# Seven-product pairs in twos with plain pairs between, nine with raw kept sums, and another order of the down-projection

## The chip, the cores and the metric

The kernel runs on one core of a Trainium2 chip. The metric is the device time of one execution in microseconds, as the median over runs. Everything is float32 at the inputs and outputs. TensorE (PE) multiplies; VectorE (DVE), ScalarE (ACT) and GpSimd (POOL) do the rest; SyncE (SP) issues most of the DMAs, and POOL some of them.

## The reference, cut to what matters

One residual block over 512 tokens of width 1024: two attention branches, their gates and projections, and then a gated convolutional feed-forward. The change touches the feed-forward, whose hidden width is 2816, and work that prepares it earlier.

```python
def conv_glu(x, w_up, conv_w, conv_b, w_down):
    hid = x @ w_up
    hid = lax.conv_general_dilated(
        hid, conv_w[:, None, :], window_strides=(1,),
        padding=((CONV_WIDTH - 1, 0),),
        dimension_numbers=('NWC', 'WIO', 'NWC'),
        feature_group_count=2 * D_FF) + conv_b
    gate, up = hid[..., :D_FF], hid[..., D_FF:]
    return (jax.nn.silu(gate) * up) @ w_down
...
        x = x + (jax.nn.sigmoid(gate_a) * (out_a @ w_branch_a[l])
                 + jax.nn.sigmoid(gate_b) * (out_b @ w_branch_b[l])) @ w_out[l]
        x = x + conv_glu(rms_norm(x, norm2_g[l]), w_ffn_up[l], ffn_conv_w[l],
                         ffn_conv_b[l], w_ffn_down[l])
```

## The kernel before

**Products in three parts.** Every float32 operand of a matmul is split into a rounded high part (a cast by ACT) and a low part (a subtraction by DVE), and each product is made as high x high + high x low + low x high. So one block of a product is three matmuls, and every weight that comes in costs a cast and a subtraction (split_gen, lines 249/250 and 278/283; split_down, lines 168/172).

**Stages.** Up to about 312 us: input projections, attention A and B, with projections as filler. Then the branch projections (yB), w_out (wo) and the second norm. From about 388 us the up-projection, from 604 us the down-projection.

**Up-projection.** The 2816 hidden columns are 22 pairs up0 to up21; pair j holds 128 gate columns and the 128 up columns that belong to them. Pairs 0 and 1 (up_first) run in halves of 256 tokens. A plain pair (up_body) is 2 x 8 x 3 = 48 matmuls of 512 columns. Twelve pairs, listed in SEVEN, are made by seven block products in place of eight (up_seven, a Strassen scheme on 2 x 2 blocks: tokens left and right, input features upper and lower half, gate and up). Each of the seven is 12 matmuls of 256 columns, so 84. The products are made in the order b1, b5, b7, b6, b1, b5, b7; after the first three ACT copies the bank into pc (L1187, L1191, L1195) so that the bank can be added to later, and DVE adds the pieces into hu and hg (L1197 to L1214). The last two matmuls of a plain pair that stands ahead of a seven-product pair are held back and run a few matmuls later (L998, L999).

The scheme needs sums of token blocks (token_sums, tiles ts, made once during pair 1) and sums of weight blocks. park_gen makes the four weight sums of each pair during attention, yB and wo: four additions on DVE (L214), then stores to a DRAM tile, parked. For a pair in SUMS the four sums are stored raw (4 DMAs of 256 KB). For another pair three of them are split first (L224 on ACT, L225 on DVE) and stored as high and low parts (7 DMAs). One call of park() makes one step, and 44 calls are spread over the attention steps, two after every group of yB and wo. In the up-projection fetch_extra brings the sums back (L237, SP's queue): 6 DMAs for a split pair; 3 for a raw one, which split_seven then splits (L249, L250). The sums go alternately into the tiles wxh/wxl and, for pairs in SECOND, w2h/w2l. split_gen fetches pair j's sums one pair early if the tile's last user stands at least three pairs before; otherwise it fetches them when the split of pair j itself begins.

**Block sums for the down-projection.** Two pairs of the up-projection form a block pair i (0 to 10). After the odd one, up_fin calls pair_sums(i): four additions on DVE, and a list rest_ with the splits into ax and ay, done by ACT and POOL's accumulating DMAs (by_dma) and followed for i < 7 by a store of ay to ayd. rest_ waits in owed until pay() is called at a fixed place of a later pair. The tile ub, from which it reads, has room for four pairs, so pair 2i + 4 writes where block pair i was. Block pairs 0 and 1 give up their ax tiles: they are stored in axd (after pairs 6 and 9) and loaded again (L1249) after pair SECOND[-1] + 1 and after the last seven-product pair + 1.

**Down-projection.** Also a seven-product scheme. A first sweep (s = 0) runs over the 11 block pairs with four products each (24 matmuls of 512 columns per block pair, L1282), a second with three (18). The weights of step i come as wd0[i] and wd1[i], one step ahead.

**What sets the order.** The program is written in one order, and a planner with a simulated timeline arranges each engine's instructions; with tc.high_priority lifts some, and behind(...) fixes the order of two. Each engine then runs its own queue in order. So a wait holds up everything behind it on its engine.

Of the kernel before, what the change touches and what calls it, by code (L numbers as in the profile page):

```python
# [15 lines left out]
P = 128  # L16
# [6 lines left out]
NP = NF // 2  # L23
# [42 lines left out]

CUTS = ((0, 256, 512, 1024, 1536, 2048), (0, 512, 1024, 1536, 2048))

SEVEN = (4, 5, 7, 8, 10, 11, 13, 14, 16, 17, 18, 20)
SUMS = (11, 13, 14, 16, 17, 18, 20)  # L70
SECOND = (5, 8, 11, 14, 17)


@with_exitstack
def block_kernel(ctx: ExitStack, tc: tile.TileContext, x, xt, params, g2, rbx, wts, wd0, wd1, out):
# [47 lines left out]
    order = [key for key, _, _ in CHUNKS]  # L123

    pos = {k: i for i, k in enumerate(order)}
    raws, splits, extras, late = {}, {}, {}, {"halves": (), "casts": (), "products": (), "pcs": ()}
    FIRST_DN = order.index("dn0_0")
    keep = {}

    def load(i):  # L130
# [15 lines left out]
        if is_seven(i):  # L146
            n = SEVEN.index(i - pos["up0"])
            SP.dma_start(raw[:, 0:512], wts[i, :, 0:512])
# [44 lines left out]
    def is_seven(i):  # L193
        return i < len(order) and order[i] in [f"up{j}" for j in SEVEN]

    def park_gen():

        for m, j in enumerate(SEVEN):
            n = SEVEN.index(j)
            i = pos[f"up{j}"]  # L200
# [779 lines left out]
    pairs = {}  # L980
# [105 lines left out]
    def up_fin(j, pg, pu, g=None):  # L1086
        if g is None:
            g = gate(j, pg)
        u = ub[:, j % 4, :]
        conv(pu, NF + j, u)  # L1090
        late["fin"] = (V.tensor_tensor(u, g, u, op=ALU.mult),)
        if j % 2 == 1 and j // 2 < 9:
            steps = pair_sums(j // 2)
            steps[0]()

            def rest_(i=j // 2):
                for step in steps[1:]:
                    step()
                if i < 7:
                    G.dma_start(ayd[i], pairs[i][1].bitcast(F32))  # L1100
            owed.append(rest_)
            if j == 17:
                owed.pop()()

    owed = []

# [2 lines left out]
    def pay():  # L1109
        if owed:  # L1110
            owed.pop()()

    def up_body(j):
        def body(hi, lo):
            pg, pu = BANK(f"pg{j}", j - 1), BANK(f"pu{j}", j - 1)
            yield from up_mm(pg, hi, lo, 0, 0, S)
            g = gate(j, pg)
            held = [] if j + 1 in SEVEN else None
            yield from up_mm(pu, hi, lo, P, 0, S, held)

            def end():
                for mm in held or ():
                    late["flip"] = (behind(mm(), late["flip"]),)
                up_fin(j, pg, pu, g)
            if held:
                late["end"] = end
            else:
                end()
            if j % 2 == 0 and j + 1 not in SEVEN:
                pay()  # L1130
        return body

# [32 lines left out]
    def up_seven(j):  # L1165
        def body(hi, lo, wh, wl):
            b1, b5, b7, b6 = [BANK(f"p{n}_{j}", j - 1 + i // 2)[:, 0:256] for i, n in enumerate((1, 5, 7, 6))]
            left, right = slice(0, 256), slice(256, 512)
            pc = fp.tile([P, 3, 256], F32, tag="pc", name=f"pc{j}")
            hg = fp.tile([P, S], F32, tag="hg", name=f"hg{j}")  # L1170
            hu = fp.tile([P, S], F32, tag="hu", name=f"hu{j}")

            def prod(ps, w, b, h, first=True, last=True):
                for k in range(4):
                    sh, sl = w[0][:, 4 * b + k, :], w[1][:, 4 * b + k, :]
                    for n, (st, mv) in enumerate(((sh, h[0]), (sh, h[1]), (sl, h[0]))):
                        mm = PE.matmul(ps, st, mv[:, k, :], start=first and k == 0 and n == 0,  # L1177
                                       stop=last and k == 3 and n == 2, skip_group_check=True)
                        behind(mm, late["pre" if late.get("end") else "flip"])
                    if late.get("end"):  # L1180
                        late["flip"] = (mm,)
                        late.pop("end")()
            r, w = (hi, lo), (wh, wl)
            B = lambda a, q: [t[:, 4 * a:4 * a + 4, q] for t in (hth, htl)]
            prod(b1, r, 0, B(0, left), last=False)
            with tc.high_priority(60):
                late["pcs"] = (A.copy(pc[:, 0], b1),)  # L1187
            yield
            prod(b5, w, 0, ts[1], last=False)
            with tc.high_priority(60):  # L1190
                late["pcs"] = (A.copy(pc[:, 1], b5),)  # L1191
            yield
            prod(b7, r, 1, ts[3], last=False)
            with tc.high_priority(60):
                third = A.copy(pc[:, 2], b7)  # L1195
            late["pcs"] = (third,)
            V.tensor_tensor(pc[:, 1], pc[:, 1], pc[:, 2], op=ALU.add)  # L1197
            yield
            if j % 2 or j + 1 not in SEVEN:
                late["copied"] = (third,)  # L1200
                pay()
            prod(b6, w, 1, ts[2])
            V.tensor_tensor(hu[:, left], b6, pc[:, 0], op=ALU.add)
            V.tensor_tensor(hu[:, right], hu[:, left], pc[:, 1], op=ALU.add)
            yield
            prod(b1, r, 2, B(1, left), first=False)
            A.copy(hg[:, left], b1)
            yield
            prod(b5, w, 2, B(1, right), first=False)
            V.tensor_tensor(hg[:, right], b5, hu[:, left], op=ALU.add)  # L1210
            g = gate(j, hg)
            yield
            prod(b7, r, 3, ts[4], first=False)
            V.tensor_tensor(hu[:, left], b7, hu[:, left], op=ALU.add)  # L1214
            up_fin(j, None, hu, g)
            yield
        return body


    halves = []  # L1220
# [19 lines left out]
    for j in range(NF):  # L1240
# [5 lines left out]
        if j in (SECOND[-1] + 1, SEVEN[-1] + 1):  # L1246
            i = int(j == SEVEN[-1] + 1)
# [20 lines left out]
    def product(s, p, i, hi, lo, ts=(0, 1)):  # L1268
        if p in ON:
            banks[p] = banks[ON[p]]  # L1270
        elif p not in banks:
            banks[p] = [ptile(tag, BUFS[tag], f"P{p}_{t}") for t, tag in enumerate(SLOTS[p])]
        a = pairs[i][s]
        h = a.shape[-1] // 2
        first, last = i == 0 and p not in ON, i == NP - 1
        for t in ts:
            o = 256 * OP[p] + P * t
            sh, sl = a[:, o:o + P], a[:, h + o:h + o + P]
            mh, ml = hi[:, BLK[p], :], lo[:, BLK[p], :]
            dst = banks[p][t]  # L1280
            for st, mv, n in ((sh, mh, 0), (sh, ml, 1), (sl, mh, 2)):
                chain("products", PE.matmul(dst, st, mv, start=first and n == 0, stop=last and n == 2,  # L1282
                                            skip_group_check=True))
# [119 lines left out]
def _layout(inputs):  # L1403
    import numpy as np
    f = {k: np.asarray(v) for k, v in inputs.items()}
    x = f["x"]
    g = f["q_norm_g"][0]
    k = f["k_norm_g"][0]
    params = np.concatenate([
        f["norm1_g"].reshape(NK, P), np.concatenate([g, g])[None], np.concatenate([k, k])[None],  # L1410
        f["ffn_conv_w"].reshape(3 * 2 * NF, P), f["ffn_conv_b"].reshape(2 * NF, P)], axis=0).T

    idx = np.clip(np.arange(639) - 127, -128, 128) + 128
    rbx = f["rel_bias"][0][:, idx]
    wts = np.empty((len(CHUNKS) - 2 * NP, P, 2048), np.float32)
    for i, (key, kn, parts) in enumerate(CHUNKS[:-2 * NP]):
        views = [f[name][0][r0:r0 + kn * P, c0:c0 + n] for name, r0, c0, n in parts]
        w = views[0] if len(views) == 1 else np.concatenate(views, axis=1)
        if key in [f"up{j}" for j in SEVEN]:

            a = w.reshape(2, 4, P, 2, P).transpose(0, 3, 2, 1, 4)
            wts[i] = np.concatenate([a[k, f].reshape(P, 512) for k in range(2) for f in range(2)], axis=1)
            continue
        wts[i] = w.reshape(kn, P, 2048 // kn).transpose(1, 0, 2).reshape(P, 2048)
        if i < 2:

            wts[i] = np.concatenate([wts[i][:, a:b].ravel() for a, b in zip(CUTS[i], CUTS[i][1:])]).reshape(P, 2048)

    w = f["w_ffn_down"][0].reshape(NP, 2, P, 2, 512)
    wd0 = np.concatenate([w[:, 0, :, 0], w[:, 1, :, 0], w[:, 0, :, 1], w[:, 1, :, 1]], axis=2)  # L1430
    wd1 = np.concatenate([w[:, 1, :, 1], w[:, 1, :, 0]], axis=2)
    arrays = {"x": x, "xt": x[0].T.reshape(NK, P, S),
              "params": params, "g2": f["norm2_g"], "rbx": rbx, "wts": wts, "wd0": wd0, "wd1": wd1}
    return {n: np.ascontiguousarray(a) for n, a in arrays.items()}
# [15 lines left out]
```

## Time and profile before

| | |
|---|---|
| median of 3 runs | 714.71 us (714.57 to 2534.47) |
| profiled execution | 714.89 us, span 713.1 us |
| up-projection, 402 to 604 us of the span | PE 201.9 us busy, DVE 171.6, ACT 138.9 |
| down-projection, 604 to 709 us | PE 105.0 us busy, DVE 88.4, ACT 46.5 |
| DMA in the whole span | 150.78 MB, 211 GB/s in the mean |

The span is from the first to the last instruction of the profiled execution, and the time given beside it has what lies around. Matmuls are pipelined, so their busy times overlap: how close PE is to its limit is read from the distance of their starts, which the chain of waits gives by its long rows (start, length, number of matmuls). A row of a group of instructions reads: line, engine, operation, written tile <- read tiles, shape, count | busy us, mean ns of one | idle time before it and what ended it.

### The profile page before, as it was taken

The numbers are of one execution on the slowest core, as the hardware profiler recorded it, in microseconds if no ns is written. First come the engines' busy times: TensorE is split into PE (matmuls) and PEld (weight loads), VectorE is DVE, ScalarE is ACT, GpSimd is POOL, SyncE is SP. The second block draws the span as 40 slices with busy tenths as digits, with TensorE's granted clock in tenths as the row PEclk, the third lists the DMA queues.
The fourth block names the chain that finished last, engine by engine and source line by source line (L and its number), as shares of the span: only waits on it lengthen the run. The fifth ranks groups of instructions, "written<-read, shape, count | busy, mean of one in ns | idle before, by whom it ended". The sixth has DMA issues, their size and how long they took to land.

```text
span 713.1 us, 11229 instructions
## 1 busy us (share of the span) xinstructions
PE 707.7 (99%) x4091; PEld 621.9 (87%) x4091; DVE 589.2 (83%) x1049; ACT 433.2 (61%) x803; POOL 81.6 (11%) x115
## 2 busy tenths in 40 slices
PE   9999999999999999999999999999999999999997
PEld 7889998888988888888889989999898988888886
DVE  6668878787999999769567988688878998989687
ACT  6576656567776776534236667677768875544531
POOL 2501200000121211000000001120222121000000
PEclk9999999999999999999999999999999999999999
DMA  8722235444434383585966647997878799564563
GB/s 315 270 99 89 78 131 183 187 162 147 179 134 162 126 296 125 206 306 195 359 232 212 229 194 222 323 314 257 259 198 253 233 265 401 209 229 168 178 214 118
DMA packets 46999, 150.78 MB, mean 211 GB/s; under 512 B 5344, under 2 KB 8032, under 8 KB 39136
## 3 DMA queue, kind: packets, MB, share of 16 engines
q1 hardware_dynamic: 40032, 131.57, 52.1%
q0 software_dynamic: 6624, 18.35, 10.0%
q8 instruction: 32, 0.52, 0.3%
q14 instruction: 23, 0.19, 0.1%
q10 hardware_dynamic: 288, 0.14, 0.1%
HBM read 114.39 MB, written 28.31 MB: 200 GB/s over the span
## 4 chain that ended last, share of the span: by engine, by line
PE 89%; DMA 4%; issue 3%; DVE 2%; ACT 1%; SPq 0%; POOL 0%; DVEq 0%; POOLq 0%; ACTq 0%
PE P L1282 15%; PE p L1177 10%; PE vA L437 3%; PE uA L437 3%; PE gB L307 2%; PE gB L308 2%; PE qkB L309 2%; PE qkB L307 2%; PE gB L309 2%; PE pg L307 2%; PE qkB L308 2%; PE pg L309 2%; PE pg L308 2%; PE wo L307 2%; PE wo L309 2%
## 5 line engine op out<-in xcount | busy, mean ns | idle before, releaser
L172 ACT CAST whi_dn<-raw_dn 128x1024 fp32r<-128x1024 f32 x33 | 34.3, 1050 | 25.4 <-PE P L1282 16.7
L1282 PE MATMUL P<-whi_dn,ax 128*128 128x512 f32 x144 | 44.5, 389 | 0.0
L168 DVE TENSOR_TENSOR wlo_dn<-raw_dn,whi_dn 128x1024 fp32r<-128x1024 f32 x33 | 40.0, 1223 | 5.1 <-ACT whi_dn L172 5.0
L1282 PE MATMUL P<-whi_dn,ay 128*128 128x512 f32 x132 | 40.8, 389 | 0.0
L741 POOL TENSOR_SCALAR_AFFINE_SELECT bB<-bB 128x128 f32<-128x128 f32 x32 | 21.8, 686 | 143.6 <-DVE bB L740 134.4
L214 DVE TENSOR_TENSOR pkr<-pkr 128x512 f32<-128x512 f32 x40 | 27.4, 685 | 8.4 <-DMA pkr<-in_wts 4.2
L1177 PE MATMUL p<-ts,whi_up 128*128 128x256 f32 x192 | 34.1, 277 | 0.0
L307 PE MATMUL pg<-hth,whi_up 128*128 128x512 f32 (+1 forms) x96 | 33.9, 354 | 0.0
L309 PE MATMUL pg<-hth,wlo_up 128*128 128x512 f32 (+1 forms) x96 | 33.9, 353 | 0.0
L308 PE MATMUL pg<-htl,whi_up 128*128 128x512 f32 (+1 forms) x96 | 33.8, 353 | 0.0
L250 DVE TENSOR_TENSOR wlo_up<-raw_up,whi_up 128x1024 fp32r<-128x1024 f32 x24 | 29.0, 1219 | 3.5 <-ACT whi_up L249 3.5
L1282 PEld LDWEIGHTS P<-whi_dn,ax 128*128 128x128 f32 x144 | 27.0, 188 | 5.6
L308 PE MATMUL pu<-htl,whi_up 128*128 128x512 f32 (+1 forms) x90 | 31.5, 350 | 0.0
L307 PE MATMUL pu<-hth,whi_up 128*128 128x512 f32 (+1 forms) x90 | 31.5, 350 | 0.0
L309 PE MATMUL pu<-hth,wlo_up 128*128 128x512 f32 (+1 forms) x90 | 31.4, 349 | 0.0
L1282 PEld LDWEIGHTS P<-whi_dn,ay 128*128 128x128 f32 x132 | 24.8, 188 | 5.1
L1177 PEld LDWEIGHTS p<-ts,whi_up 128*128 128x128 f32 x192 | 29.0, 188 | 0.1
L739 DVE TENSOR_TENSOR_SCAN aB<-aB,reset 128x127 f32<-128x127 f32 (+3 forms) x32 | 25.9, 816 | 2.6 <-ACT aB L734 2.5
L1282 PE MATMUL P<-wlo_dn,ax 128*128 128x512 f32 x72 | 28.0, 389 | 0.0
L1177 PE MATMUL p<-hth,whi_up 128*128 128x256 f32 x96 | 26.7, 278 | 0.1
L249 ACT CAST whi_up<-raw_up 128x1024 fp32r<-128x1024 f32 x24 | 24.6, 1051 | 3.5 <-PE pu L308 2.8
L1177 PE MATMUL p<-hth,wlo_up 128*128 128x256 f32 x96 | 26.5, 276 | 0.0
(349 smaller groups left out, 2537.9 us busy)
## 6 DMA issues: line engine op xcount, KB each, us to landing
parked<-pkr SPq DMA_DIRECT2D x45, 256.0 KB, 2.7
raw_dn<-in_wd SPq DMA_DIRECT2D x11, 1024.0 KB, 4.9
pkr<-in_wts SPq DMA_DIRECT2D x10, 1024.0 KB, 6.9
raw_up<-in_wts SPq DMA_DIRECT2D x10, 1024.0 KB, 5.7
raw_up<-in_wts SPq DMA_DIRECT2D x12, 512.0 KB, 6.9
raw_dn<-in_wd SPq DMA_DIRECT2D x11, 512.0 KB, 3.6
wxl_up<-parked SPq DMA_DIRECT2D x21, 256.0 KB, 5.6
ayd<-ay POOLq DMA_DIRECT2D x7, 768.0 KB, 7.1
```

The costliest lines, as they stand in the source:

```text
L168: chain("halves", V.tensor_tensor(o, x, y, op=op))
L172: chain("casts", A.copy(hi[:, sl], src))
L214: V.tensor_tensor(b[o], b[x], b[y], op=op)
L249: behind(A.copy(h[:, sl], src[:, sl]), late["pcs"])
L250: V.tensor_tensor(l[:, sl], src[:, sl], h[:, sl].bitcast(F32), op=ALU.subtract)
L307: ins = PE.matmul(ps, sh, mh, start=first, stop=False)
L308: PE.matmul(ps, sh, ml, start=False, stop=False)
L309: PE.matmul(ps, sl, mh, start=False, stop=last)
L437: PE.matmul(pss[t], st[:, 4 * half + k, t * P:(t + 1) * P], mv[:, k, :], start=half == 0 and k == 0 and j == 0, stop=half == 1 and k == 3 ...
L739: V.tensor_tensor_scan(ar, ar, reset[:, S - n:S - 1][:, ::-1], 1.0, op0=ALU.mult, op1=ALU.max)
L1177: mm = PE.matmul(ps, st, mv[:, k, :], start=first and k == 0 and n == 0, stop=last and k == 3 and n == 2, skip_group_check=True)
L1282: chain("products", PE.matmul(dst, st, mv, start=first and n == 0, stop=last and n == 2, skip_group_check=True))
```

## The change

Three edits. The twelve seven-product pairs are put at other places: always two in a row with a plain pair between, then 18 and 20 alone. Nine of them keep raw sums in place of seven (SUMS), so three are split ahead in place of five; SECOND follows the new places. The conditions under which rest_ is paid follow the new places, and the call that paid it at once after pair 17 goes. In the down-projection a table DOWN puts block pair 2 ahead of 0 and 1; the host lays the weights out in that order. The number of seven-product and of plain pairs stays, and so does every product.

```diff
-SEVEN = (4, 5, 7, 8, 10, 11, 13, 14, 16, 17, 18, 20)
-SUMS = (11, 13, 14, 16, 17, 18, 20)
-SECOND = (5, 8, 11, 14, 17)
+SEVEN = (3, 4, 6, 7, 9, 10, 12, 13, 15, 16, 18, 20)
+SUMS = (7, 9, 10, 12, 13, 15, 16, 18, 20)
+SECOND = (4, 7, 10, 13, 16)
+
+
+DOWN = (2, 0, 1, 3, 4, 5, 6, 7, 8, 9, 10)
...
-    raws, splits, extras, late = {}, {}, {}, {"halves": (), "casts": (), "products": (), "pcs": ()}
+    raws, splits, extras, late = {}, {}, {}, {"halves": (), "casts": (), "products": (), "pcs": (), "flip": ()}
...
             owed.append(rest_)
-            if j == 17:
-                owed.pop()()
...
-            if j % 2 == 0 and j + 1 not in SEVEN:
+            if j == 18 or j < 18 and j % 2 == 0 and j + 1 not in SEVEN:
                 pay()
...
-            if j % 2 or j + 1 not in SEVEN:
+            if j == 18 or j < 18 and (j % 2 or j + 1 not in SEVEN):
                 late["copied"] = (third,)
                 pay()
...
-        a = pairs[i][s]
+        a = pairs[DOWN[i]][s]
...
-    w = f["w_ffn_down"][0].reshape(NP, 2, P, 2, 512)
+    w = f["w_ffn_down"][0].reshape(NP, 2, P, 2, 512)[list(DOWN)]
```

## The prediction

> **What bounds the kernel now.** I read the page first (shares of the span, then the slices), then the chain of work that ended last, then who makes TensorE's weight loads wait, and last the busy times by stretch.
>
> ```profile
> span 713.1 us, 11229 instructions
> PE 707.7 (99%) x4091; PEld 621.9 (87%) x4091; DVE 589.2 (83%) x1049; ACT 433.2 (61%) x803; POOL 81.6 (11%) x115
> ```
>
> The profiled execution took 714.89 us, so 1.8 us lie around its span of 713.1; the median of the runs shown is 714.71, 0.18 lower. PE is busy for all but 5.4 us. Busy matmuls can still be far apart, so the chain has to show whether they follow each other without gaps:
>
> ```profile
> 423.21 0.35 PE p L1177 x3
> 424.04 18.71 PE p L1177 x165
> 453.19 0.35 PE p L1177 x3
> 454.02 18.71 PE p L1177 x165
> ...
> 524.79 10.58 DMA wxl_up<-parked
> ...
> 548.79 0.35 ACT pc L1187
> 549.18 20.99 PE p L1177 x180
> 570.41 2.73 PE p L1177 x24
> ...
> 604.28 104.94 PE P L1282 x462
> 709.25 0.42 DVE x__7105 L1287
> ```
>
> In the double of seven-product pairs 4 and 5 (from 424.04) 165 matmuls of 256 columns take 18.71 us, 113.4 ns each. In the down-projection 462 matmuls of 512 columns take 104.94 us, 227.1 ns each. Twice the columns cost twice the time, so PE streams columns without a break. A seven-product pair (84 matmuls) is 84 x 113.4 = 9.5 us, a plain pair (48 of 512 columns) 48 x 227.1 = 10.9 us. The one stretch that isn't clean begins at 549.18, inside pair 16 of the run 16, 17, 18: 180 matmuls should take 18.71 + 15 x 0.1134 = 20.41 us and take 20.99, 0.58 us too long. Just before it, the last matmul before 549.18 starts at 548.81 and should have been followed 0.11 us later: 0.26 us more.
>
> ```profile
> 548.81 0.28 PE L1177 MATMUL p<-ts,wxl_up 128*128 128x256 f32 x1
> 549.18 0.39 PE L1177 MATMUL p<-hth,whi_up 128*128 128x256 f32 x1
> ```
>
> ```profile
> PEld gA L307 <- DVE mixA L626: 0.5, 1, 0.5
> PEld P L1282 <- DVE wlo_dn L168: 0.3, 1, 0.3
> PEld p L1177 <- ACT pc L1187: 0.3, 1, 0.3
> ```
>
> These waits agree: in the whole up-projection only one is listed, for ScalarE's copy of the first product (pc, L1187). So what the change can win there is about 0.58 + 0.26 = 0.84 us, and everything else must come from matmuls that it does not remove.
>
> **The change part by part.**
>
> *TensorE's work.* Twelve pairs by seven products before and after, ten plain ones before and after; the diff touches no product. The sum is 0. The pairs stand as 3 4 | 6 7 | 9 10 | 12 13 | 15 16 | 18 | 20 in place of 4 5 | 7 8 | 10 11 | 13 14 | 16 17 18 | 20, so there is one more turn from a plain to a seven-product pair. At such a turn three matmuls of 256 columns and the two held ones of 512 stand between 423.21 and 424.04: 3 x 0.1134 + 2 x 0.2271 = 0.79 us in 0.83. One more turn: +0.04 us.
>
> *The run of three goes.* The stall at 548.81 is the end of a delay of the helpers, not of PE: ScalarE sat for the kept sums of pair 16, whose transfer took 10.58 us (524.79 in the chain).
>
> ```profile
> ACT wxh_up L249 <- DMA wxl_up<-parked: 6.3, 2, 5.4
> wxl_up<-parked SPq DMA_DIRECT2D x21, 256.0 KB, 5.6
> w2l_up<-parked SPq DMA_DIRECT2D x15, 256.0 KB, 8.8
> ```
>
> After the change the last pairs are 15 16, plain 17, 18, plain 19, 20. Pair 18 then has another non-SECOND pair (15) three places before it, so the rule in split_gen fetches its sums early; in the old order 16 stood two places before and the fetch had to wait. The rest_ of block pair 8 is no longer forced out at once after pair 17, between two seven-product pairs, but paid in 18. What is late next is unknown; the doubles at 424.04 and 454.02, with the same 165 matmuls in 18.71 us, show that a double between plain pairs runs clean. I take all of it: -0.84 us; the bounds are -0.84 and 0 (the loss only moves).
>
> *Two more pairs keep raw sums* (9 for 7; parked already split are 3, 4, 6 for 4, 5, 7, 8, 10).
>
> ```profile
> L225 DVE TENSOR_TENSOR pkr<-pkr,pkh 128x512 fp32r<-128x512 f32 x10 | 6.9, 686 | 0.5 <-ACT pkh L224 0.3
> L224 ACT CAST pkh<-pkr 128x512 fp32r<-128x512 f32 x10 | 6.2, 620 | 6.0 <-DMA parked<-pkh 3.6 <-DVE pkr L225 2.1 <-DVE pkr L214 0.3
> L250 DVE TENSOR_TENSOR wxl_up<-wxl_up,wxh_up 128x1024 fp32r<-128x1024 f32 x4 | 4.9, 1221 | 4.6 <-ACT wxh_up L249 4.6
> L250 DVE TENSOR_TENSOR wxl_up<-wxl_up,wxh_up 128x512 fp32r<-128x512 f32 x4 | 2.7, 685 | 0.0
> L249 ACT CAST wxh_up<-wxl_up 128x1024 fp32r<-128x1024 f32 x4 | 4.2, 1046 | 5.4 <-DMA wxl_up<-parked 5.4
> L249 ACT CAST wxh_up<-wxl_up 128x512 fp32r<-128x512 f32 x4 | 2.5, 619 | 0.9 <-DMA wxl_up<-parked 0.9
> ```
>
> Removed from the attention stage: 2 x 3 casts of 0.62 (3.7 us of ACT), 2 x 3 subtractions of 0.686 (4.1 us of DVE), 2 x 3 stores of 256 KB on SP's queue, and four calls of park(), so the last sums are ready two groups earlier. Added in the up-projection: 2 x (1.221 + 0.685) = 3.8 us of DVE, 2 x (1.046 + 0.619) = 3.3 us of ACT. Removed there: 2 x 3 fetches of 256 KB on SP's queue (1.5 MB, 5 to 6 us at the 276 GB/s of the stretch below). The cover for the added work:
>
> ```profile
> 200.00:220.00 20.00, 20.00 (x104) 16.85 (x104) 19.90 (x38) 14.43 (x33) 3.58 (x6) 1.00 0.41 152
> 402.00:432.00 30.00, 30.00 (x171) 26.27 (x170) 26.63 (x42) 17.23 (x27) 0.73 (x1) 1.00 0.48 176
> 432.00:604.00 172.00, 171.90 (x1223) 160.22 (x1223) 144.92 (x226) 121.71 (x206) 33.67 (x43) 1.00 0.90 276
> 604.00:709.00 105.00, 105.00 (x464) 86.53 (x462) 88.39 (x115) 46.52 (x58) 1.05 (x2) 1.00 0.54 188
> ```
>
> The columns are stretch, length, busy PE, PEld, DVE, ACT, POOL, clock, DMA share and GB/s. From 432 to 604 DVE has 172 - 144.92 = 27.1 us free, 23.3 with the added 3.8; ACT has 50.3, 47.0 after. The DMA engines, 0.90 busy, are relieved. If that cover were gone, each microsecond of it would stop PE; with it, 0. In the attention stage DVE is full (19.90 of 20 at 200 to 220) and loses 4.1 us there, but the first three parked pairs are split as before, so the 0.5 us wait of gA L307 near 121 us stays, and PE shows no other wait for DVE there. I take -0.1, between 0 and -0.9 (that engine's lateness may hide in many small gaps).
>
> *Sevens begin one pair earlier.* Pair 3 starts at about 423.2 - 10.9 = 412.3 and needs the token sums and its own fetched sums.
>
> ```profile
> L237 SPq DMA_DIRECT2D w2l_up<-parked x15: 319/430/1409, 392.3 to 532.3; - x15
> L1161 DVE TENSOR_TENSOR ts<-x,ts x4: 1214/1216/1224, 394.7 to 403.6; 128x1024 fp32r<-128x1024 f32 x4
> 413.68 2.36 DVE L250 TENSOR_TENSOR wlo_up<-raw_up,whi_up 128x1024 fp32r<-128x1024 f32 x2 [2.29 <-ACT whi_up L249]
> 428.60 1.22 DVE L250 TENSOR_TENSOR wlo_up<-raw_up,whi_up 128x1024 fp32r<-128x1024 f32 x1
> ```
>
> The last token sum starts at 403.6 and takes 1.2 us, 7.5 us before 412.3: 0. The sums of the first two such pairs are fetched as soon as the feed-forward pool exists (the second pair's from 392.3, landing 8.8 us later), for 3 and 4 now in place of 4 and 5, and all is there by about 404: 0. Pair 3 by seven products adds five DVE steps of 0.42 us, 2.1 us, to 402 to 432, where DVE is free for 3.4 us, of which 2.29 are spent waiting at 413.68 for the weight buffer. So 1.0 us of the 2.1 may not fit. Pair 5's last split ends at 428.60 + 1.22 = 429.8, and PE reached pair 5 at about 423.2 + 0.5 + 9.5 = 433.2 (pair 4 and the two held matmuls): 3 us of slack against 1.0. I take 0; the bounds are 0 and +2.1.
>
> *pay() and the first-half sums.* rest_ for pairs 0 to 8 is paid in 3, 4, 7, 9, 10, 13, 15, 16, 18 (2, 5, 7, 8, 11, 13, 14, 17, 17 before): the same steps on ACT and POOL, two of them in one double at 3 4, 9 10 and 15 16, as before in 7 8 and 13 14. 0 on PE. Where it adds a wait it is on ACT, which writes ub again one pair later; behind it stand pc's copies, which PE needs three products (36 x 0.1134 = 4.1 us) after they are due.
>
> *Down-projection.* Block pair 2 is read first; it was never stored away. Block pairs 0 and 1 come back by a load:
>
> ```profile
> L1249 SPq DMA_DIRECT2D ax0b<-axd x1: 319/319/319, 561.9 to 561.9; - x1
> L1249 SPq DMA_DIRECT2D ax1b<-axd x1: 319/319/319, 586.7 to 586.7; - x1
> DMA to landing us min/median/max: 5.0/5.0/5.0
> ```
>
> ax0b has landed 37 us before the first product at 604.28, and ax1b 18 us before the second block pair (24 matmuls of 0.2271 us later, 609.7). Taking pair 2 first gives each one or two steps more of slack that was not needed: 0 us. The weights are put in the same order on the host, outside the time.
>
> The sum against the profiled execution: 714.89 + 0.04 - 0.84 - 0.1 = 713.99, about 714.0 us. I keep 714.0 for the median; the 0.18 between the two lies inside the range.
>
> **A rule to weigh.** The Trainium skill (Perfetto Trace Analysis, Identifying the Most-Contended Engine) says that TensorE's matmul busy share is no measure of its headroom and that the busy share of weight loads is. By that rule PE's 87% leaves 713.1 - 621.9 = 91 us; by the row of 104.94 us for 462 matmuls it leaves nothing in the down-projection, where weight loads are busy for only 86.53 of 105 us. The measured spacing decides here, and the rule is the ground of the rival on the fast side.
>
> **The rivals.**
>
> (B) The loss only moves. The delayed transfer of kept sums hits another double, with raw sums now also in 7, 9, 10. For it: 0.90 of the DMA time is used, and two rest_ still fall in one double. Against it: 1.5 MB less is fetched, and pair 16's neighbour 18 is gone. Time: 714.89 + 0.04, up to 0.3 more: 714.6 to 715.2. The change would then do nothing that shows.
>
> (C) A new wait in the first double, the case of the other sign. DVE comes out of the token sums late, and 1.0 to 2.1 us of its work does not fit before pair 5; PE waits for the second half of pair 5's weights or for a bank. It decides once the lateness passes the 3 us of slack above. Time: 714.0 + 1.0 to 2.1 = 715.0 to 716.1.
>
> (D) Kept sums are late for each pair. If PE had to wait at all nine raw pairs, 14.3 us (2%) would need 1.6 us each. One transfer of 10.58 us makes this thinkable; the seven raw pairs of before, with 0.84 us lost in all, speak against it. Time: above 729.
>
> (E) PE is not the bound, and relieved helpers let it run nearer to its weight loads. The 60 or so us between 621.9 and the end would open in part: below 700. No stretch shows matmuls closer than 113.4 ns per 256 columns.
>
> (F) The attention stage gains more than I count, from 4.1 us less on a full DVE: 712.5 to 713.4.
>
> **How the numbers follow.** My forecast (A: the loss of the run of three goes, nothing new above 0.4 us) 0.55; its own range is 713.5 to 714.5. B 0.24, C 0.12, F 0.05, D 0.03, E 0.01. The range from 713.1 to 715.8 holds A, B, the lower half of C and a little of F, some 0.85; it reaches down by the 0.9 us of the attention stage and up into C. About 2% of 714.7 (14.3 us) is what a measurement of this kernel can tell from no change by the bound used here; only D reaches it upward and only E downward: faster 0.01, same 0.96, slower 0.03.
>
> **What would show it.** Right: 4091 matmuls; no gap above 0.2 us in PE's starts between pairs 15 and 20; down-projection again 462 matmuls in about 104.9 us; L249/L250 on the kept sums 18 each in place of 14; L224/L225 9 each in place of 15. Wrong: a wait of PE for pc, for wlo_up or for wxl_up in any double (B, D), one between 412 and 433 us (C), a shorter spacing than 113.4 ns (E). If the median is below 713.1 or above 715.8, a term that I set at 0 is not 0.

## The result and the profile after

The changed kernel took 727.76 us (median of 4 runs, 723.71 to 1841.13), the kernel before 714.87 beside it: a ratio of 1.0152 with a 95% interval of 1.0115 to 1.019. The forecast was 714.0 with a range up to 715.8, so the change cost some 12 us that the prediction does not have. The profile taken with these runs is of the execution of 1841 us, in the slow state; below, "after" is a second look at the same kernel (run e1: median 726.85 us; profiled execution 727.32, span 725.6). In the changed file the lines from L214 on stand 3 lower, and those from L1177 to L1282 one lower: L237, L249, L987, L1064 and L1177 are now L240, L252, L990, L1067 and L1178.

The head of its page:

```profile
span 725.6 us, 11199 instructions
PE 712.2 (98%) x4091; PEld 624.2 (86%) x4091; DVE 589.5 (81%) x1047; ACT 431.5 (59%) x801; POOL 81.9 (11%) x115
```

The same 4091 matmuls, and the helpers are no busier: DVE, ACT and POOL have the totals of before to within 2 us. PE is busy 4.5 us longer (it runs slower for a while, see below) in a span that is 12.5 us longer. No work was added. Work waits, so the next view is who made PE wait. This is the list of waits between 402 and 625 us (waiting engine, tile and line, releaser: sum in us, times, longest):

```profile
ACT wxh_up L252 <- DMA wxl_up<-parked: 13.3, 4, 6.0
ACT ub L990 <- DMA ax<-ub: 6.9, 2, 3.6
PEld p L1178 <- ACT pc L1188: 5.7, 4, 2.5
```

Before, the first row had 6.3 us and the last one 0.3. PE now waits four times for pc, ScalarE's copy of the first product, and ScalarE waits for kept sums and for ub. PE's own instructions at the two worst places (start, length; in brackets the idle time before it and what ended it):

```profile
510.86 0.28 PE L1178 MATMUL p<-ts,wxl_up 128*128 128x256 f32 x1
512.94 0.39 PE L1178 MATMUL p<-hth,whi_up 128*128 128x256 f32 x1 [1.81 <-ACT pc L1188]
...
575.46 0.28 PE L1178 MATMUL p<-ts,wxl_up 128*128 128x256 f32 x1
578.07 0.38 PE L1178 MATMUL p<-hth,whi_up 128*128 128x256 f32 x1 [2.34 <-ACT pc L1188]
```

Both stops stand between the fourth and the fifth product of pairs 12 and 18: the fifth is b1 again, and it needs the bank that pc has to copy away. The next start should come 0.11 us later; it comes 2.08 and 2.61 us later, so 1.97 and 2.50 us are lost. Before, exactly this step had lost 0.26 us at 548.81.

Each of the two stops is followed by a second loss. The columns are stretch, length, busy PE, PEld, DVE, ACT and POOL, clock, DMA share, GB/s:

```profile
510.21:513.62 3.41, 1.60 (x14) 1.41 (x13) 1.92 (x4) 2.29 (x4) 0.00 (x0) 1.00 0.98 207
513.62:517.03 3.41, 3.41 (x18) 3.41 (x17) 3.41 (x5) 3.41 (x8) 0.56 (x1) 0.50 0.34 138
575.06:578.47 3.41, 1.07 (x9) 0.88 (x9) 1.95 (x3) 2.01 (x4) 0.00 (x0) 1.00 0.94 261
578.47:581.88 3.41, 3.41 (x18) 3.41 (x18) 3.38 (x5) 2.77 (x7) 0.00 (x0) 0.50 0.05 9
```

In the 3.41 us behind each stop the granted clock is 0.50. The starts of the matmuls stand 0.213 us apart in place of 0.113, so 16 start where 30 would (x18 counts all that reach into the stretch). By these distances the half clock costs another 1.60 and 1.57 us.

The attention stage has two new stops as well (waits between 200 and 402 us; before, PE had none there):

```profile
PEld pT_B L760 <- POOL bB L744: 1.5, 1, 1.5
PEld yB L310 <- DVE gb L872: 1.3, 1, 1.3
```

Adding up the distances of PE's starts against the clean spacing (0.1134 us per 256 columns) gives where the span grew, in us:

| place | before | after |
|---|---|---|
| attention and yB, at 248 and 323 us | 0 | 1.40 + 1.03 |
| up-projection, fifth products at 480, 511, 545, 575 us | 0.27 (549) | 0.32 + 1.97 + 0.79 + 2.50 |
| half clock behind two of these | 0 | 1.60 + 1.57 |
| first steps of the down-projection, 621 us | 0 | 0.76 |
| sum | 0.27 | 11.9 |

The table leaves out losses under 0.2 us. So 11.7 of the 12.5 us have a place. 8.5 of them, the clock included, are in the up-projection, and every stop there is the same step in the first pair of a double or in 18 (pairs 9, 12, 15, 18).

Why is ScalarE late for pc? The kept sums of pair 12 show it. First POOL's accumulating DMAs and SP's fetch, then ScalarE, all of after:

```profile
485.14 0.84 POOL L1067 DMA_DIRECT2D ay<-st  x1 [11.27 <-ACT ax L1066]
...
489.07 0.84 POOL L1067 DMA_DIRECT2D ax<-ub  x1 [1.30 <-ACT cg L990]
```

```profile
488.04 2.13 SPq L240 DMA_DIRECT2D wxl_up<-parked  x3
```

```profile
497.58 1.05 ACT L252 CAST wxh_up<-wxl_up 128x1024 fp32r<-128x1024 f32 x1 [5.00 <-DMA wxl_up<-parked]
```

The four DMAs that split block pair 3 are issued from 485.14 to 489.07, in pair 9, the first of a double. The three transfers of the kept sums start at 488.04, in the middle of them; the chain of waits gives the transfer 9.87 us (from 489.59). ScalarE's queue has come to the cast of these sums and stands for 5.00 us; behind it are the convolutions of pairs 10 and 11 and the copy pc of pair 12. The same picture stands at 549.75 to 553.77 (block pair 6, paid in 15) with the sums of pair 18, where ScalarE stands 5.96 us.

The reason is one condition. rest_ is paid after an even plain pair j only if j + 1 is not in SEVEN. The new plain pairs inside the pattern are 2, 5, 8, 11, 14, 17, 19; the even ones, 2, 8 and 14, all stand ahead of a seven-product pair. So it never holds, and block pairs 3 and 6 wait for 9 and 15.

The single stall of before shows the same rows, seen now that the pattern is known:

```profile
520.29 0.86 POOL L1064 DMA_DIRECT2D ay<-st  x1 [9.99 <-ACT ax L1063]
...
523.96 0.85 POOL L1064 DMA_DIRECT2D ax<-ub  x1 [1.06 <-issue]
```

```profile
523.33 2.21 SPq L237 DMA_DIRECT2D wxl_up<-parked  x3
```

There, too, a rest_ was paid in the first pair of a double (13), and the fetch for pair 16 went out among POOL's four DMAs and took 10.58 us. No run tests whether they caused that stall.

### The profile page after: what moved, and what is told of

The parts are those of the page before. It is cut to its first block, busy times and chain, and to the rows that moved or that the text cites. A ratio compares the mean times of both kernels' runs of the same rounds, so it can differ in the third digit from the quotient of the medians.

```text
span 1839.4 us, 11199 instructions
## 1 busy us (share of the span) xinstructions
PE 1834.3 (100%) x4091; PEld 1313.2 (71%) x4091; DVE 603.6 (33%) x1047; ACT 439.1 (24%) x801; POOL 76.3 (4%) x115
## 4 chain that ended last, share of the span: by engine, by line
PE 100%; DVE 0%; DVEq 0%; issue 0%
PE p L1178 16%; PE P L1283 15%; PE vA L440 3%; PE uA L440 3%; PE pg L311 3%; PE pg L310 3%; PE pg L312 3%; PE pu L311 2%; PE pu L310 2%; PE pu L312 2%; PE gA L311 2%; PE qkB L310 2%; PE wo L311 2%; PE gB L311 2%; PE wo L312 2%; PE gB L312 2%
## 5 line engine op out<-in xcount | busy, mean ns | idle before, releaser
L1283 PE MATMUL P<-whi_dn,ax 128*128 128x512 f32 x144 | 102.7, 828 | 0.0
L1283 PE MATMUL P<-whi_dn,ay 128*128 128x512 f32 x132 | 94.1, 829 | 0.0
L1178 PE MATMUL p<-ts,whi_up 128*128 128x256 f32 x192 | 78.9, 529 | 0.0
L1178 PEld LDWEIGHTS p<-ts,whi_up 128*128 128x128 f32 x192 | 70.3, 433 | 1.4 <-issue 1.4
L1283 PE MATMUL P<-wlo_dn,ay 128*128 128x512 f32 x66 | 54.6, 828 | 0.0
L311 PE MATMUL gA<-htl,whi_gA 128*128 128x512 f32 x64 | 54.0, 844 | 0.0
L311 PE MATMUL qkB<-htl,whi_qkB 128*128 128x512 f32 x64 | 53.9, 842 | 0.0
L310 PE MATMUL qkB<-hth,whi_qkB 128*128 128x512 f32 x64 | 53.8, 840 | 0.0
L312 PE MATMUL gB<-hth,wlo_gB 128*128 128x512 f32 x64 | 53.7, 839 | 0.0
L310 PE MATMUL gB<-hth,whi_gB 128*128 128x512 f32 x64 | 53.6, 838 | 0.0
L311 PE MATMUL gB<-htl,whi_gB 128*128 128x512 f32 x64 | 53.6, 837 | 0.0
```

The costliest lines, as they stand in the source:

```text
L310: ins = PE.matmul(ps, sh, mh, start=first, stop=False)
L311: PE.matmul(ps, sh, ml, start=False, stop=False)
L312: PE.matmul(ps, sl, mh, start=False, stop=last)
```

## The experiments

The ratio is always to the kernel before, run on the same chip beside it (715.15 to 715.71 us), with its 95% interval. Differences in us between runs on different chips can be off by the half microsecond between these medians. Stops named in passing are of the one profiled execution of a run.

### Which of the three edits: e1 to e4

e1 is the changed kernel once more.

> The changed kernel once more, to have a profile at full clock. Three theories for the 9 to 13 us that it is longer than before. Attention theory: with two pairs' sums stored raw the planner lays out the attention stage otherwise from the fourth parked pair on, and PE waits there; the loss then lies between 200 and 400 us of the span, and the up-projection is clean. Early-double theory: VectorE is late out of the token sums and PE waits at pairs 3 to 5; the loss lies between 402 and 440 us. Raw-sums theory: PE waits for pieces of kept sums in several doubles; the loss is spread over 440 to 604 us in pieces of 1 us and more. All expect 722 to 728 us, the granted clock a little under 1.0 near the place of the loss, and a down-projection of 104.9 us.

726.85 us, 1.0158 (1.0139 to 1.0178). The loss is real and not one of the first runs alone. The early-double theory is out, since PE has no stop between 402 and 480 us; each of the other two has a part, as the table above shows.

e2 has only the two more raw sums, at the old places (SUMS in the kernel before):

```diff
-SUMS = (11, 13, 14, 16, 17, 18, 20)
+SUMS = (8, 10, 11, 13, 14, 16, 17, 18, 20)
```

> The old places and the old order of the down-projection, but nine pairs with raw kept sums (8 and 10 besides the seven). Attention theory: 722 us or more, the loss at the same place as in the changed kernel. Early-double theory: as before, 714 to 716 us. Raw-sums theory: 716 to 722 us, with waits of PE in the doubles of 8 and 10.

720.83 us, 1.0067 (1.0046 to 1.0089). PE stops at 248 us (1.41) and 323 us (0.73), as in after, once for long in a double (1.48, in pair 13, not in 8 or 10 as was expected), and twice at the turn to the down-projection (0.75 + 0.77); no half clock. So raw sums alone cost some 5 to 6 us, 2.1 of them in the attention stage.

e3 has the new places, the new conditions and DOWN, with seven raw sums:

```diff
-SUMS = (7, 9, 10, 12, 13, 15, 16, 18, 20)
+SUMS = (10, 12, 13, 15, 16, 18, 20)
```

> The new places, payments and down-projection order, but seven pairs with raw kept sums as before (7 and 9 are stored split), so that the program up to the up-projection is the same as before. Attention theory: 713 to 716 us. Early-double theory: 722 us or more, as the changed kernel. Raw-sums theory: 716 to 720 us.

721.99 us, 1.0099 (1.0078 to 1.0119). The stops in the attention stage are gone, and those in the doubles stay: 1.62 us in pair 15, 1.89 us in pair 18, then 2.6 us at the turn. So both edits cost, in different stages. The time is what the early-double theory said, but not the place.

e4 is the kernel before with DOWN alone:

```diff
+DOWN = (2, 0, 1, 3, 4, 5, 6, 7, 8, 9, 10)
...
-        a = pairs[i][s]
+        a = pairs[DOWN[i]][s]
```

> The kernel before with the new order of the down-projection alone. The same instructions in the same order on every engine but PE, where block pair 2 is read first. All theories: as before, 714 to 715.5 us, down-projection 104.9 us.

715.60 us, 1.0007 (0.9997 to 1.0018). The order of the down-projection neither costs nor gains that can be told from 0.

### Is it the late payment: e5, e6, e11, e12

e6 is the changed kernel with one condition edited, so that block pairs 3 and 6 are paid in the plain pairs 8 and 14:

```diff
-            if j == 18 or j < 18 and j % 2 == 0 and j + 1 not in SEVEN:
+            if j in (8, 14):
                 pay()
```

> The changed kernel, but the same block sums are paid one pair earlier, inside the plain pairs 8 and 14; nothing else is touched. Collision theory: their DMAs are over when the fetch for 12 and 18 starts, 718 to 722 us, no stall above 1 us at pairs 12 and 18. Rival (too much work for ScalarE and VectorE in a double): 723 us or more, since the same work is only moved ahead. The stalls at about 248 and 322 us stay in both.

716.20 us, 1.0006 (0.9994 to 1.0019): one line takes away 10.7 of the 11.7 us, more than either theory had. Its waits, 402 to 625 us:

```profile
ACT wxh_up L252 <- DMA wxl_up<-parked: 1.6, 1, 1.6
ACT ub L990 <- DMA ax<-ub: 1.1, 1, 1.1
```

13.3 and 6.9 us have become 1.6 and 1.1, PE waits for no pc at all, the up-projection is clean, and the clock stays at 1.00. The transfer itself shows what changed. Issues between 476 and 512 us (KB each, median us from issue to landing), after and then e6:

```profile
wxl_up<-parked SPq DMA_DIRECT2D x3, 256.0 KB, 8.9
```

```profile
wxl_up<-parked SPq DMA_DIRECT2D x3, 256.0 KB, 3.1
```

In e6 the fetch goes out at 483.53, 4.5 us sooner, when POOL's DMAs for block pair 3 are all but through (the last lands at 484.50). The Trainium skill (DMA: Bandwidth & Descriptors, SWDGE vs HWDGE vs iDMA) says that transfers issued by GpSimd and by the other engines enter different queues of the same DMA engines, which serve them in turn. By that rule sharing with POOL's DMAs lengthens the fetch, and the rows agree in direction. They don't give its price, because the order on SP's queue differs too, in after and then in e6:

```profile
486.50 0.33 SPq L151 DMA_DIRECT2D raw_up<-in_wts  x1
486.88 0.56 SPq L152 DMA_DIRECT2D raw_up<-parked  x1
487.49 0.51 SPq L153 DMA_DIRECT2D raw_up<-in_wts  x1
488.04 2.13 SPq L240 DMA_DIRECT2D wxl_up<-parked  x3
```

```profile
483.53 1.28 SPq L240 DMA_DIRECT2D wxl_up<-parked  x3
485.46 0.33 SPq L151 DMA_DIRECT2D raw_up<-in_wts  x1
```

In after the fetch stands behind three loads of raw weights (1 MB), in e6 ahead of them. Behind the same three loads, but with no DMA of POOL beside it, the fetch of before at 492.87 took 5.0 us. As an estimate from these three rows, of the 5.8 us between 3.1 and 8.9 some 2 belong to the loads ahead and 4 to POOL's DMAs.

What remains of e6's loss is in the attention stage (1.66 + 0.43 us at 248 and 323).

e5 keeps the payment in 9 and 15 but splits block pairs 3 and 6 without DMAs, by the casts and subtractions that block pair 0 uses:

```diff
-        if 0 < i < 9:
+        if 0 < i < 9 and i not in (3, 6):
             return sums, by_dma
...
-        if i == 0:
+        if i in (0, 3, 6):
             return sums, lambda: halves(ax, ax_parts()), lambda: halves(ay, ay_parts())
```

> The changed kernel, but the block sums of pairs 3 and 6 (those paid inside the first pair of a double) are split by ScalarE and VectorE in place of POOL's accumulating DMAs; the result is the same. Collision theory: these DMAs share the DMA engines with the fetch of kept sums for pairs 12 and 18, the sums land late, ScalarE stands at their cast and PE at the copy pc; without them the two long stalls (2.0 and 2.5 us, each with a stretch at half clock) fall under 1 us: 717 to 721 us, granted clock 1.0. Rival, ScalarE and VectorE simply have too much to do in a double: VectorE gets 2 x 2.5 us more, so 726 us or more.

716.46 us, 1.001 (0.9996 to 1.0025), a little below the range, and the up-projection is clean. That would show the DMAs as the cause, but by_dma also costs ScalarE a negated copy of each part (L1066, 0.84 + 0.63 + 0.42 + 0.42 = 2.3 us per block pair), which e5 takes away too. behind(..., late["copied"]) holds these copies until the double has begun. e11 separates the two: it keeps the negated copies, overwritten by the subtraction, and takes away only the DMAs.

```diff
-                G.dma_start(a[:, n + o:n + sl.stop].bitcast(F32), src, accum_op=ALU.add)
+                if i not in (3, 6):
+                    G.dma_start(a[:, n + o:n + sl.stop].bitcast(F32), src, accum_op=ALU.add)
                 A.copy(a[:, sl], src)
+                if i in (3, 6):
+                    V.tensor_tensor(a[:, n + o:n + sl.stop], src, a[:, sl].bitcast(F32), op=ALU.subtract)
```

> The changed kernel; only for block pairs 3 and 6 (paid in 9 and 15) POOL's accumulating DMAs are replaced by subtractions on DVE, and all three-part work of ACT stays as it is (in the run that took both away, ACT had 2 x 2.3 us less to do). If the collision of these DMAs with the transfers of the kept sums and with ub's reuse is the cause: the up-projection as clean as there, 715.5 to 718, no wait of ACT for kept sums above 3.5 us and no half clock. Rival: ACT's own extra work in the double was what made it late: stops of PE near 510 and 575 us remain, 721 to 728.

720.82 us, 1.0065 (1.0043 to 1.0088): neither theory's number. The waits of e11, 402 to 625 us:

```profile
ACT wxh_up L252 <- DMA wxl_up<-parked: 8.0, 4, 3.0
ACT ub L990 <- DMA ax<-ub: 5.5, 2, 3.3
PEld p L1181 <- ACT pc L1191: 1.5, 1, 1.5
PEld P L1286 <- ACT whi_dn L175: 1.4, 1, 1.4
```

Without the DMAs the longest wait for kept sums falls from 6.0 to 3.0 us, the stops at 511 and 575 us and the half clock go, and 6.0 of the 11.7 us. (Up to 1 us of that may be the stop at 323 us, which this execution does not have although the program is the same up to there.) But ScalarE is still late: a stop of 1.47 us at 540, and 1.9 us at the turn to the down-projection. Without the copies as well (e5) another 4.4 us go. So the late payment hurts in two ways of like size: by its DMAs, and by its copies, which stand in ScalarE's queue inside the double. How the DMAs do it is only partly seen: the fetch for pair 18 has become shorter (its last two transfers 6.1 and 5.3 us in place of 10.0 and 9.9), but the one for pair 12 still takes 8.4 us with POOL's store ayd<-ay beside it; it goes out 1.9 us sooner. My expectation that the DMAs alone explain it was wrong.

e12 pays only block pair 3 early:

```diff
-            if j == 18 or j < 18 and j % 2 == 0 and j + 1 not in SEVEN:
+            if j == 8:
                 pay()
```

> The changed kernel with block pair 3's rest_ alone paid in plain pair 8 (block pair 6's stays in 15). If each of the two late payments makes its own stop: the stop near 510.9 us (1.97 us and the half clock behind it) goes, the one near 575 us stays: 720 to 723.5. Rival: lateness carried on from the first makes both: about 716, both stops gone. Second rival: block pair 6's is the whole of it: above 725.

720.83 us, 1.0074 (1.0059 to 1.0089). Its waits:

```profile
ACT wxh_up L252 <- DMA wxl_up<-parked: 8.5, 4, 6.3
PEld P L1283 <- ACT whi_dn L175: 1.7, 1, 1.7
PEld P L1283 <- DVE wlo_dn L171: 1.0, 1, 1.0
PEld p L1178 <- ACT pc L1188: 0.7, 1, 0.7
```

The time is that of "each payment makes its own stop", but the places are not. ScalarE still stands 6.3 us for the sums of pair 18, and yet PE stops only 0.62 us there; the rest comes out later, as 0.60 us at 594 and 2.3 us at the turn. So the 2.5 us stop of after at 575 needed lateness carried over from the first payment. A wait of ScalarE is not a stop of PE of a fixed size: what slack is left decides.

### The sums' price, and a kernel better than both: e7, e8

e7 is e6 with the seven raw sums of e3.

> As the run before, with seven pairs' sums raw, so that everything up to the up-projection is as in the kernel before. Collision theory: 714.5 to 717 us; the stalls at 248 and 322 us are gone and those in the doubles under 1 us. Rival: 719 us or more.

713.82 us, 0.997 (0.9959 to 0.998): below the expected range, and 0.3% faster than the kernel before. Its chain ends in

```profile
603.26 104.93 PE P L1283 x462
```

where the down-projection had started at 604.28 before. No wait of PE is listed between 200 and 625 us, and the span is 712.1 us. Against e3 it differs in one line and is 8.2 us faster; against e6 in two raw sums, 2.4 us faster.

e8 pays still earlier, at every even pair (the second condition; the first is as in e7):

```diff
-            if j == 18 or j < 18 and (j % 2 or j + 1 not in SEVEN):
+            if j == 3 or j % 2 == 0 and j < 20:
```

> As the run before, but every block sum is paid in the pair right after its own (4, 6, 8 and so on), evenly two pairs apart. Collision theory: 714 to 718 us, if none of them now falls on a fetch; the one paid at 12 could meet the fetch for 15 and cost up to 2 us. Rival: 719 us or more.

714.04 us, 0.9982 (0.9969 to 0.9995). The up-projection is as clean, so nothing more is to be had there.

### Two that limit the explanation: e9, e10

e9 makes the collision in the kernel before, by paying block pairs 4 and 7 one pair sooner, in the first pair of a double:

```diff
-            if j % 2 or j + 1 not in SEVEN:
+            if j in (10, 16) or j not in (11, 17) and (j % 2 or j + 1 not in SEVEN):
```

> The kernel before, with its old places, but the block sums of pairs 4 and 7 are paid inside the first pair of a double (10 and 16) in place of the second (11 and 17). Collision theory: their DMAs now meet the fetch of kept sums for pairs 13 and 18, as in the changed kernel; stalls of 1 us and more at the first product's copy in 13 or 18, 717 to 722 us. Rival (the new places are what costs): 714.5 to 716 us.

715.59 us, 1.0004 (0.9992 to 1.0016). That is the rival's time: the expected loss did not come, although the collision did:

```profile
ACT wxh_up L249 <- DMA wxl_up<-parked: 12.5, 5, 5.0
PEld p L1177 <- ACT pc L1187: 1.1, 1, 1.1
```

ScalarE waits 12.5 us for kept sums, as in after (13.3), but never for ub, and PE's longest stop is 1.1 us even in the profiled execution, which was the slowest of ten (717.8 us). So at the old places a late fetch alone is not enough. In after, ScalarE loses another 6.9 us to ub: plain pairs 8 and 14 write it while the DMAs of block pairs 2 and 5, paid in 7 and 13, still read it. That this makes the difference is argued, not tested.

e10 changes only the order of ScalarE's casts in after: the kept sums come behind both raw pieces.

```diff
-            parts[1:1] = [(wh, wl, wl.bitcast(F32), slice(0, 1024))]
-            parts += [(wh, wl, wl.bitcast(F32), slice(1024, 1536))]
+            parts += [(wh, wl, wl.bitcast(F32), slice(0, 1024))]
+            parts += [(wh, wl, wl.bitcast(F32), slice(1024, 1536))]
```

> The changed kernel, payments as it has them, but the casts of the kept sums stand last in each pair's split, behind both pieces of the raw weights. If the cost is that ScalarE, in order, stands at a cast whose sums have not landed while work for PE waits behind it, the casts now come later, the stalls at pairs 12 and 18 shrink by half or more: 719 to 723 us. If the late landing itself stops PE (the second product needs the sums), the time stays at 725 us or more, and PE waits for wxh or wxl in place of pc.

722.30 us, 1.0105 (1.0087 to 1.0124), 4.6 us less than after with the same transfers at the same places. The stops at 511 and 575 us go; one at 540 us, of pair 15, grows from 0.79 to 2.32 us:

```profile
ACT ub L990 <- DMA ax<-ub: 6.4, 2, 3.9
PEld p L1178 <- ACT pc L1188: 2.4, 1, 2.4
```

The wait for ub is left: ScalarE stands 3.9 us for it until 540.74, just ahead of that pc, with no wait for kept sums beside it. So the place of a waiting cast in an in-order queue counts as much as the transfer that it waits for.

## Why the prediction was wrong

**What bounds the kernel** was read rightly: PE's spacing is as before (153 matmuls in 17.35 us in the double of after, 113.4 ns each), so every microsecond lost is a stop or a stretch at half clock.

**The run of three goes, -0.84 us**: right in kind, somewhat too large. The 0.58 in it is misread: the chain's row of 180 matmuls reaches 0.16 us into a matmul of 512 columns of pair 19 (from 570.01). By the distances of the starts 0.42 us were lost there, so 0.69 in all. In e7, the change with its payments placed well and seven raw sums, the loss is gone. Its down-projection starts 1.02 us earlier than before's, but 0.47 of that is there already at 397 us, where both run the same program; the up-projection gained 0.55, against 0.84 - 0.04 = 0.80. By the medians on one chip e7 gained 1.76 us (715.58 to 713.82); where the rest lies the traces don't show. The cause named for the stall was at best half of it. The prediction's argument on early fetching is about pair 18, while the stall was in pair 16. That POOL's four DMAs stood from 520.29 to 523.96 beside pair 16's fetch at 523.33 was in the trace and was not looked for.

**"0 on PE" for pay() and the first-half sums** is the step that failed, and the largest. The prediction wrote the places down (two payments in a double at 3 4, 9 10, 15 16), counted them as "the same steps", and compared them with 7 8 and 13 14 of before. It did not ask which transfers run beside them in the new order: of 13 14, one stood beside the fetch ahead of the only stall of before. It even named the chain (ScalarE's wait stands ahead of pc, 4.1 us of slack), but set no price, where a single row of before (5.37 us of ScalarE's time for one such fetch) exceeds the slack. Measured: 10.7 us (e1 against e6), of them 3.2 by the clock in the profile.

**Two more raw sums**: the cover in the up-projection held where the payments stood well (e6 is clean there with nine), but not at the old places: e2 has stops of 1.48, 0.32 and 0.54 us there. The attention stage was taken at -0.1 us, between 0 and -0.9, from 4.1 us less work on DVE. It cost 2.4 us instead (e6 against e7, 716.20 and 713.82). There are fewer steps, but they stand elsewhere, and one engine's order decides. At 248 us POOL's mask of bB waits for a subtraction on DVE that now stands behind sums for parking and weight splits. At 323 us it is this (DVE, before and after):

```profile
316.89 2.87 DVE L214 TENSOR_TENSOR pkr<-pkr 128x512 f32<-128x512 f32 x4 [2.15 <-DMA pkr<-in_wts]
```

```profile
320.46 2.87 DVE L217 TENSOR_TENSOR pkr<-pkr 128x512 f32<-128x512 f32 x4 [4.49 <-DMA pkr<-in_wts]
```

DVE stands 4.49 us for a weight load that is only parked for later, and gb, which yB's next bank needs, is queued behind it. How much of it reaches PE differs between kernels that are the same up to there (0 in e11, 0.43 us in e6, 1.03 in after, 1.67 in e5), by when the load goes out: at 310.92 us in e11 and 314.18 in e5, where DVE waits 2.33 and 5.13 us for it.

**Sevens one pair earlier, 0; DOWN, 0**: right. PE has no stop between 402 and 480 us in after, and e4 is at 1.0007, with a stop of 0.58 us early in the down-projection of its profile that e7, with the same DOWN, does not have.

**The rivals.** B had the mechanism, a late fetch that meets another double, and priced it at 0.3 us, the size that the one stall of before had left after its slack. C did not happen. D was too high, E showed nothing (the 60 us in it should be the 91 of the rule), and F had the wrong sign. The range was too narrow because it treated a collision as a term with a price; near the end of the slack it has none: 12.5 us of the same wait came with 1.5 us of stops in the up-projection of e9, and 13.3 us with 8.5, clock included, in after.

What stays open: the share of ub's reuse in the up-projection was not separated from the other two. A second ub buffer, which would do it, was not tried. Nor does any run hold the order on SP's queue fixed: e5, e6 and e12 have the fetch for pair 12 ahead of the loads of raw weights, after, e3, e10 and e11 behind them. That order alone does not make the stop at 511 us, since e3, e10 and e11 do not have it.

## What to carry to other kernels

When work moves to another step, list which transfers will be in flight there and what is queued behind each wait, step by step; equal counts of the same steps say nothing. A condition such as "pay here unless the next one is special" has to be walked through for the new list, since it can quietly never hold. And removing work from a stage that an in-order schedule has packed can make it slower, because the order around it changes.

## What the runs showed of the hardware

A stop of PE can cost nearly double through the clock: that of 1.97 us was followed by another 1.60. The two drops of after begin at 513.62 and 578.47 us, 64.85 us or 19 x 3.413 us apart, and each lasts 3.413 us: the clock is granted in windows on a fixed grid. Counted on that grid, here are the window with the stop and the one behind it in e10, and then in e3:

```profile
538.82:542.23 3.41, 1.37 (x13) 1.18 (x11) 0.68 (x1) 1.49 (x4) 0.00 (x0) 1.00 0.59 231
542.23:545.64 3.41, 3.29 (x15) 3.29 (x16) 3.27 (x5) 3.41 (x7) 0.00 (x0) 0.50 0.01 2
```

```profile
537.39:540.80 3.41, 1.95 (x17) 1.76 (x16) 1.76 (x3) 2.71 (x6) 0.00 (x0) 1.00 0.37 153
540.80:544.21 3.41, 3.41 (x31) 3.41 (x31) 3.41 (x6) 3.41 (x8) 0.24 (x1) 1.00 0.11 11
```

Of the windows inside PE's work, over all profiles that record the clock, three were followed by half clock, with matmuls busy for 1.07, 1.37 and 1.60 us; the least busy one that was not had 1.95 us. But the window in which e3's matmuls end (714.88 to 718.30) was busy for 1.60 us too, and the clock behind it stayed full. So the limit lies near half a window, at 1.6 to 1.95 us of 3.413, and these modelled busy times place it no closer. Whether a stop of 2 us crosses it depends on whether it falls into one window or over two: e3's longest, 1.89 us at 570.21, was cut by a window's edge and cost no clock.

The Trainium skill (TensorE: Matmul & The Clock Gate, What's actually happening) gives the same free-running window, 3413 ns, and has the clock fall after at least one idle window; its advice (Why this matters for your kernels) is to keep stops under about 3 us. The window agrees with the 3.413 us here. The limit does not: a stop of 1.97 us, in a window in which PE was busy for 1.60 us, was enough.
